# Stored partial sums loaded beside the gate tiles, and a regrouped staging of the output projection, in a hybrid retention and S5 layer

## The chip, the cores and the metric

The kernel runs on one core of a Trainium2 chip. The metric is the device time of one execution in microseconds (us): the median of three timed runs of the kernel before is 2620.29 us (2620.25 to 2623.68).

## The reference, cut to what matters

One layer serves 1024 prompt tokens and 8 sample tokens, 1032 columns in all. After an RMS norm one wide projection gives queries, keys, values, two S5 inputs and four gates. Two branches (retention and a diagonal state space) work on them, and the end of the layer, where the change lies, is

```python
yb = y * jax.nn.sigmoid(y @ w_glu + b_glu)            # inside the S5 branch
ya = (ya * silu(za)) @ w_pa                           # 1024 -> 2048
yb = (yb * silu(zb)) @ w_pb                           # 1024 -> 2048
merged = jax.nn.sigmoid(ga) * ya + jax.nn.sigmoid(gb) * yb
out = merged @ w_out                                  # 2048 -> 2048
return x + rmsnorm(out, g_post)
```

All of it is float32 (2048 wide model, 8 retention heads of 128, 64 S5 groups of 16).

## The kernel before, in words

**Products.** The big matrix products go over 2x2 blocks with seven products in place of eight: `product(g)` (L907) is one of them, `g // 7` is the step and `g % 7` the product in it. A step makes two row blocks of 128 outputs over a depth of 1024 (512 for each block of the 2x2 scheme). Each float32 operand is split into a high and a low float32r part (ACT copies the high part, DVE subtracts), and three matmuls stand for one. So a step before the output projection is 7 x 24 matmuls of 258 columns, and a step of the output projection is 7 x 12 of 324.

**Steps.** Steps 0 to 69 are the two depth halves of the wide projection, 70 to 73 `glu` (SG = 70), 74 to 81 `pa` (SA = 74), 82 to 89 `pb` (SB = 82), 90 to 97 and 98 to 105 the two depth halves `o0` and `o1` (SO = 90, SP = 98) of the output projection for the last 648 columns (TA = 384 to TOK = 1032). The first 384 columns follow in a last loop (from L1724) that uses the merged columns as the stationary operand and 512 wide pieces of `w_out`.

**Forms.** The right hand side of the seven products are seven forms of four tiles each (`FORMS`, L751). Three are parts of the source itself (`u1`, `v1`, `v2`), four are sums (`t1` to `t4`) that an earlier piece of work stores in device memory: `make_forms` (L1393) for `pb`, `forms_o` (L1480) for the output projection, which loads pairs of rows of `mg_d`, makes four DVE operations on each pair and stores two tiles to `fo_d`. `transition` (L1301) then loads ("stages") the 28 form tiles of a stage of work, one tile a DMA (`stage`, L840), and splits them (`unstage`, L859, through `split`, L258) during the last three steps before they are used: two loads in each of the first four products, as many as the pool `stg3` has buffers, then a load behind each split. The places `a0` to `a15` rotate (`qslot`, L828), and `forms_o` uses two places that are free meanwhile (`a6`, `a7` for `o0`; `a4`, `a5` for `o1`), two pairs of rows at a time, so the third and fourth pair overwrite the first and second.

**Gates.** In `pa` and `pb` an evacuated result tile `t` (128x516) is multiplied by its gate (`gated`, L1429), which `load_z` (L1423) has loaded on ACT's queue into `zz`. `pa` stores the product in `pap_d` (L1448). `pb` has DMA add `pap_d` into `t` (L1450, an accumulating DMA on POOL's queue) and four products later (LAG = 4) stores `t` to `mg_d` (L1451), also by POOL.

**Tiles in flight.** The evacuation tiles `p1`, `u2` and `u3` come from the pool `ev` with two buffers each, `st` from another with two; PSUM has three accumulators (`pst`). The weights `wr` come through SP's queue (`fetch`, L864) into seven buffers; `prep` (L880) forms the block sums and the splits two products ahead.

**What sets the order.** Each engine works through one list in order, and a wait at its head holds all behind it. The tile framework makes these lists from the program, and may bring an instruction forward past others of its engine; `issue_after` binds the background work (`slot`, `late_work`) only to instructions on PE, ACT, DVE and SP. POOL has no such anchor.

**The last loop.** `load_m` (L1528) loads 384 columns of a row of `mg_d`, `split_m` (L1531) splits them and loads the row four further; the first four loads are written at the start of the last step, the splits follow, one a product and then one a pass of the last loop. The norm weights `gb` and the residual rows `x_of(0)`, 1 MB each, are loaded by POOL ahead of that loop (L1702, L1703).

Of the kernel before, what the change touches and what calls it, by code (L numbers as in the profile page):

```python
# [10 lines left out]
F32 = mybir.dt.float32  # L11
# [7 lines left out]
D = 2048  # L19
SEQ = 1024  # L20
NB = 8
TOK = SEQ + NB
# [6 lines left out]
SW = TOK - TA  # L29
HO = SW // 2  # L30
THIRDS = [(0, 384), (384, 768), (768, TOK), (TA, TOK)]
HT = TOK // 2
# [47 lines left out]
def emit(ctx, tc, I, O):  # L80
    nc = tc.nc
    V, A, P, T = nc.vector, nc.scalar, nc.gpsimd, nc.tensor
# [7 lines left out]
    def add(out, a, b, eng=None):  # L90
        return tt(out, a, b, ALU.add, eng)
# [19 lines left out]
    act = ctx.enter_context(tc.tile_pool(name="act", bufs=1))  # L111
# [19 lines left out]
    pap_d = dram("pap_d", [16, 128, TOK])  # L131
# [16 lines left out]
    mg_d = dram("mg_d", [16, 128, TOK])  # L148
# [19 lines left out]
    bg = deque()  # L168
# [129 lines left out]
    def x_of(k):  # L298
        return xs[k][:, 0, :], xs[k][:, 1, :]
# [50 lines left out]
    with tc.tile_pool(name="start", bufs=3) as sp:  # L350
        ssq = sp.tile([128, TOK], F32, name="ssq", bufs=1)
        banks = [[mmbank() for _ in range(3)], [mmbank(), mmbank(), misc()]]
        w = None
# [449 lines left out]
    def popen(name, side, bufs):  # L803
        st = ExitStack()
        return st, st.enter_context(tc.tile_pool(name=name, bufs=bufs, side=side))
# [11 lines left out]
    lim = [7 * len(steps)]  # L817
# [117 lines left out]
    def at(g, f):  # L935
        due.setdefault(g, []).append(f)
# [359 lines left out]
        opened["fx"], opened["fxp"] = popen("fx", "left", 4)  # L1296

    def stg_open(bufs):
        opened["stg"], opened["stgp"] = popen("stg3", "left", bufs)

    def transition(g, base, kind, eng=P):  # L1301

        q = g - 7 * base
        n = moved.setdefault(kind, [0, 0])

        def load(eng=P):
            at(g, lambda o=order_q[n[0]]: stage(opened["stgp"], kind, *o, eng))
            n[0] += 1

        if 0 <= q < 4:  # L1310
            load(eng)
            load(eng)
        if 3 <= q < 20:
            for i in range(1 if q < 7 else 2):
                if n[1] < 28:
                    at(g, lambda o=order_q[n[1]]: unstage(kind, *o))
                    n[1] += 1
                    if n[0] < 28:
                        load()
# [73 lines left out]
    def make_forms(src, F):  # L1393

        t = {}

        def ld(i):
            t[i] = [opened["fxp"].tile([128, TOK], F32, name="fx") for _ in range(2)]
            for x, k in zip(t[i], (i, 4 + i)):
                P.dma_start(x, src[k])  # L1400

        ld(0)
        ld(1)
        for _ in range(3):
            yield
        for i in range(4):
            u, v = t.pop(i)
            mix_a(u, v)
            yield
            mix_b(u, v, F, i)  # L1410
            yield
            if i < 2:
                yield
                yield
                ld(i + 2)
                yield
        opened["fx"].close()


    zq = {}  # L1420
    AT = {"11": (0, 0), "22": (1, 1), "21": (1, 0), "12": (0, 1)}

    def load_z(s, name):  # L1423
        kind, p = steps[s]
        r, c = AT[name]
        zq[name] = zz_tile()
        A.dma_start(zq[name], {"glu": zy_d, "pa": sga_d, "pb": sgb_d}[kind][2 * p + r, :, HT * c:HT * c + HT])

    def gated(g, name, t, ps=None):  # L1429
        s = g // 7  # L1430
        kind, p = steps[s]
        r, c = AT[name]
        m, cols = 2 * p + r, slice(HT * c, HT * c + HT)
        z = zq.pop(name)
        if kind == "glu":
            def times():
                mul(t, t, z)
                P.dma_start(yb_d[m, :, cols], t)

            A.activation(t if ps is None else two(t), t if ps is None else ps, AF.Sigmoid, bias=bglu[:, m:m + 1])  # L1440
            at(g + 1, times)
            return
        if ps is None:
            mul(t, t, z)
        else:
            mul(two(t), ps, two(z))
        if kind == "pa":
            P.dma_start(pap_d[m, :, cols], t)  # L1448
        else:
            P.dma_start(t, pap_d[m, :, cols], accum_op=ALU.add)  # L1450
            at(g + LAG, lambda: P.dma_start(mg_d[m, :, cols], t))  # L1451
# [28 lines left out]
    def forms_o(kh, wait):  # L1480

        t, w = {}, {}

        def ld(i):
            if i < 2:
                w[i] = act.tile([128, 2, TOK], F32, name=f"a{(6, 4)[kh] + i}")
            t[i] = w[i % 2][:, 0, 0:SW], w[i % 2][:, 1, 0:SW]
            for x, k in zip(t[i], (8 * kh + i, 8 * kh + 4 + i)):
                P.dma_start(x, mg_d[k, :, TA:TOK])

        for i in range(4):
            if i % 2 == 0:
                if i:
                    yield
                ld(i)
                if i:
                    yield
                ld(i + 1)
                for _ in range(wait):
                    yield  # L1500
            u, v = t.pop(i)
            u1, u2, v1, v2 = u[:, 0:HO], u[:, HO:SW], v[:, 0:HO], v[:, HO:SW]
            sub(u1, u1, u2)
            sub(u2, u2, v2)
            yield
            add(v2, v2, u1)
            sub(v1, v1, v2)
            P.dma_start(fo_d[kh, 0, i], u)
            P.dma_start(fo_d[kh, 1, i], v)
            yield  # L1510

    flat_ = {}

# [14 lines left out]
    def load_m(m):  # L1528
        P.dma_start(spare(m), mg_d[m, :, 0:TA])

    def split_m(m):  # L1531
        split(merged(m), spare(m))
        if m + 4 < KD:
            load_m(m + 4)
# [121 lines left out]
    for s in range(SG, len(steps)):  # L1656
        kind, p = steps[s]
        if s in (SG + 1, SA + 1, SB + 1, SO + 1, SP + 1):
            opened["stg"].close()
        if s == SA + 1:  # L1660
            fx_open()
            bg.append(make_forms(yb_d, fb_d))
        if s == SB + 4:
            bg.append(forms_o(0, 2))
        if s in (SG + 2, SB - 2, SB + 6, SP - 2):
            drain()
            stg_open(8)
        if s == SO:
            zstack.close()
            bg.append(forms_o(1, 3))  # L1670
        if s == SO + 1:
            zrstack, zr0 = popen("zr", "left", 4)
            zrp = [zr0]
        if s == SP + 1:
            zr2stack, zr1 = popen("zr2", "left", 4)
            zrp.append(zr1)
            bg.append(rows_out())
        for n in range(7):
            g = now[0] = 7 * s + n
            if n == 1:  # L1680
                fetch(s + 1)
            prep(g + 2)
            (evac_p if s < SO else evac_o)(g, product(g))
            if n in (0, 2, 3, 4) and s < SO:
                at(g, lambda s=s, n=n: load_z(s, {0: "11", 2: "22", 3: "21", 4: "12"}[n]))
            transition(g, 2 * NP - 2, "glu")
            transition(g, SG + 2, "pa")
            transition(g, SB - 2, "pb")
            transition(g, SB + 6, "o0")
            transition(g, SP - 2, "o1")  # L1690
            if s == len(steps) - 1 and n > 4:
                raw_of["pool"] = wst
                next_w()
            if s == len(steps) - 1:
                for m in range(4) if not n else (n - 1,):
                    at(g, lambda m=m, n=n: split_m(m) if n else load_m(m))
            late_work(g)
            slot()
    small = const.tile([128, 24], F32, name="small")
    sm = [(small[:, o:o + 4], small[:, o + 4:o + 5], small[:, o + 5:o + 6], small[:, o + 6:o + 7]) for o in (0, 8, 16)]  # L1700
    gb = flat(1, "gb")[:, 0:D]
    P.dma_start(gb, bass.AP(tensor=I["g_post_row"].tensor, offset=I["g_post_row"].offset, ap=[[0, 128], [1, D]]))  # L1702
    P.dma_start(x_of(0), I["xB"][0])  # L1703

    def evac_c(g, c, ps):
        s4, r1, r2, r3 = sm[c]
# [17 lines left out]
    for g in range(4):  # L1724
        both_ = banks_of["pst"].tile([128, 2, 512], F32, name="acc")
        ps = [both_[:, 0, :], both_[:, 1, :], mmbank()]
        e = 11 if g == 3 else 13
        todo_ = [[(k, c) for c in range(3)] for k in range(e)] + [[(k, c) for k in range(e, KD)] for c in range(3)]
        for st in todo_:
            for k, c in st:  # L1730
                while order_w and order_w[0] <= (g, k + 1):
                    next_w()
                wh, wl = wb[g, k]
                xh, xl = (a[:, 128 * c:128 * c + 128] for a in merged(k))
                for a, b in ((xh, wh), (xh, wl), (xl, wh)):
                    anchor["p"] = T.matmul(ps[c], a, b, start=k == 0 and a is xh and b is wh, stop=k == KD - 1 and a is xl).ins  # L1736
                if k == KD - 1:
                    evac_c(g, c, ps[c])
            now[0] += 1
            if rest:  # L1740
                with ExitStack() as after:
                    for ins in anchor.values():
                        after.enter_context(tc.issue_after(ins))
                    split_m(rest.popleft())
            slot()
        if g == 2:
            drain()
# [81 lines left out]
```

## Time and profile before

| what | value |
|---|---|
| median of three runs | 2620.29 us |
| the profiled execution | 2619.01 us, span 2617.1 us |
| granted TensorE clock | 0.994 |
| PE busy, weight loads busy | 2565.9 us (98%), 2518.0 us (96%) |
| DVE, ACT, POOL busy | 1983.2 us (76%), 971.5 us (37%), 784.4 us (30%) |
| DMA moved | 519.09 MB, mean 198 GB/s |

The span runs from the first to the last instruction of the profiled execution; its own time is 1.9 us more. PE is busy in nearly all of the 40 slices of the profile but for two about 2200 us in (0.8 and 0.7) and the last (0.8). In the rows of the profile an engine's name with a q is its sequencer; the releaser of a wait is inferred from the semaphores.

### The profile page before, as it was taken

The page shows a single profiled execution, that of the slowest core. Times are in us where ns is not written, and L with a number is a line of the kernel's source. Part 1 is how long each engine was busy: PE and PEld are TensorE (multiplying, and loading weights), DVE is VectorE, ACT ScalarE, POOL GpSimd, SP SyncE. Part 2 cuts the span into 40 slices and gives each one's busy share as a digit, 9 for nine tenths or more (in the row PEclk, how much of TensorE's full clock was granted, in tenths as well). Part 3 has the DMA queues.
Part 4 walks back from the last instruction along what each step waited for, and adds up shares of the span by engine and source line. Part 5 has one row for each costly group of instructions (what it writes and reads, how often), then busy time and mean ns, then how long its engine had stood idle before and what let it go on. Part 6 is the DMA issues. An engine that isn't in the chain of part 4 may idle for free.

```text
span 2617.1 us, 52507 instructions
## 1 busy us (share of the span) xinstructions
PE 2565.9 (98%) x19948; PEld 2518.0 (96%) x19948; DVE 1983.2 (76%) x4159; ACT 971.5 (37%) x1747; POOL 784.4 (30%) x1300
## 2 busy tenths in 40 slices
PE   9999999999999999999999999999999998799998
PEld 8999999999999999999999999999999998799976
DVE  6655988889889877558877766668886866788875
ACT  6113233333323324343333444346532422345532
POOL 0103322222222222333244444335221323523320
PEclk9999999999999999999999999999999999999999
DMA  5886434434444447888879888889786879957784
GB/s 192 265 267 209 151 115 127 138 119 120 133 122 128 131 138 236 205 208 198 201 200 247 228 205 227 203 207 298 248 275 236 249 197 249 275 174 175 196 303 139
DMA packets 233500, 519.09 MB, mean 198 GB/s; under 512 B 33968, under 2 KB 61056, under 8 KB 232480
## 3 DMA queue, kind: packets, MB, share of 16 engines
q0 software_dynamic: 106464, 308.09, 42.9%
q1 hardware_dynamic: 91552, 159.30, 19.8%
q10 hardware_dynamic: 35232, 48.36, 5.9%
q8 instruction: 157, 2.57, 0.4%
q14 instruction: 95, 0.78, 0.1%
HBM read 342.36 MB, written 173.25 MB: 197 GB/s over the span
## 4 chain that ended last, share of the span: by engine, by line
PE 81%; issue 6%; DMA 6%; DVE 3%; POOL 3%; ACT 1%; POOLq 0%; DVEq 0%; ACTq 0%; SPq 0%
PE acc L919 63%; PE acc L1736 5%; PE mm L214 2%; PE mm L212 2%; PE mm L213 2%; DMA u<-pap_d 1%; DMA fo_d<-a 1%; DVE a L85 1%; DMA a<-mg_d 1%; DMA st<-pap_d 1%; PE misc L637 1%; PE misc L715 1%; PE misc L714 1%; DVE wlo L85 1%; PE misc L1133 1%
## 5 line engine op out<-in xcount | busy, mean ns | idle before, releaser
L919 PE MATMUL acc<-a,whi 128*128 128x258 f32 (+1 forms) x10976 | 1844.0, 287 | 30.9 <-DVE u L85 22.3
L919 PEld LDWEIGHTS acc<-a,whi 128*128 128x128 f32 x10976 | 1545.2, 190 | 39.3 <-ACT whi L900 12.2
L919 PE MATMUL acc<-a,wlo 128*128 128x258 f32 (+1 forms) x5488 | 1156.8, 285 | 0.5 <-DVE wlo L85 0.5
L919 PEld LDWEIGHTS acc<-a,wlo 128*128 128x128 f32 x5488 | 866.9, 190 | 1.0 <-DVE wlo L85 1.0
L900 ACT CAST whi<-wraw 128x512 fp32r<-128x512 f32 x424 | 263.2, 621 | 690.0 <-PE acc L919 512.4
L85 DVE TENSOR_TENSOR wlo<-wraw,whi 128x512 fp32r<-128x512 f32 x456 | 312.7, 686 | 173.3 <-ACT whi L900 114.2
L900 ACT CAST whi<-wr 128x512 fp32r<-128x512 f32 x318 | 197.3, 621 | 567.3 <-PE acc L919 511.1
L85 DVE TENSOR_TENSOR wlo<-wr,whi 128x512 fp32r<-128x512 f32 x380 | 260.7, 686 | 72.7 <-ACT whi L900 41.7
L212 PE MATMUL mm<-a,whi 128*128 128x384 f32 (+1 forms) x448 | 145.1, 326 | 5.6 <-ACT whi L205 5.6
L85 DVE TENSOR_TENSOR wraw<-wr 128x512 f32<-128x512 f32 x212 | 145.5, 686 | 2.7
L213 PE MATMUL mm<-a,whi 128*128 128x384 f32 (+1 forms) x448 | 145.2, 324 | 0.1
L214 PE MATMUL mm<-a,wlo 128*128 128x384 f32 (+1 forms) x448 | 144.8, 323 | 0.1
L85 DVE TENSOR_TENSOR a<-stg,a 128x516 fp32r<-128x516 f32 (+1 forms) x196 | 118.0, 632 | 32.2 <-ACT a L259 27.9
L259 ACT CAST a<-stg 128x516 fp32r<-128x516 f32 (+1 forms) x196 | 104.8, 574 | 48.5 <-DMA stg<-mg_d 17.8
L1736 PE MATMUL acc<-whi,a 128*128 128x512 f32 x372 | 117.8, 395 | 1.9 <-ACT whi L205 1.9
L85 DVE TENSOR_TENSOR u<-acc,p 128x516 f32<-128x516 f32 (+1 forms) x106 | 70.1, 661 | 57.3 <-PE acc L919 56.7
L85 DVE TENSOR_TENSOR u<-acc,u 128x516 f32<-128x516 f32 (+1 forms) x100 | 67.3, 673 | 58.7 <-PE acc L919 57.7
L85 DVE TENSOR_TENSOR p<-acc,p 128x516 f32<-128x516 f32 (+1 forms) x100 | 67.2, 672 | 53.3 <-PE acc L919 53.2
L973 POOL DMA_DIRECT2D u<-pt_d x70 | 61.6, 881 | 117.7 <-DVE u L85 79.5
L85 DVE TENSOR_TENSOR u<-p,acc 128x516 f32<-128x516 f32 (+1 forms) x106 | 69.7, 657 | 32.5 <-PE acc L919 12.9
L971 POOL DMA_DIRECT2D pt_d<-u x70 | 38.6, 552 | 179.7 <-DVE u L85 129.7
L212 PEld LDWEIGHTS mm<-a,whi 128*128 128x128 f32 x448 | 84.5, 189 | 5.8 <-ACT whi L205 5.6
(395 smaller groups left out, 3080.8 us busy)
## 6 DMA issues: line engine op xcount, KB each, us to landing
wr<-in_w_in SPq DMA_DIRECT2D x280, 256.0 KB
pt_d<-u POOLq DMA_DIRECT2D x70, 258.0 KB, 3.1
u<-pt_d POOLq DMA_DIRECT2D x70, 258.0 KB, 5.0
wr<-in_w_out SPq DMA_DIRECT2D x64, 256.0 KB
wr<-in_w_outB SPq DMA_DIRECT2D x64, 256.0 KB
stg<-fm_d POOLq DMA_DIRECT2D x44, 258.0 KB, 4.4
pt_d<-st POOLq DMA_DIRECT2D x35, 258.0 KB, 3.2
pt_d<-p POOLq DMA_DIRECT2D x35, 258.0 KB, 3.1
```

Of the source, the lines that this page charges most:

```text
L85: return (eng or V).tensor_tensor(out, a, b, op)
L212: T.matmul(ps, wh[:, i, :], xh[:, t0:t1], start=first, stop=False)
L213: T.matmul(ps, wh[:, i, :], xl[:, t0:t1], start=False, stop=False)
L214: anchor["p"] = T.matmul(ps, wl[:, i, :], xh[:, t0:t1], start=False, stop=last).ins
L259: A.copy(dst[0], src)
L637: T.matmul(ps[0:16, g * 128:(g + 1) * 128], B1[:, g, :], W3[:, g, 0:8, :], start=True, stop=True)
L714: T.matmul(o, Tm[:, g, :], U[:, g, 0:136], start=True, stop=False)
L900: anchor["a"] = A.copy(hi, f).ins
L919: anchor["p"] = T.matmul(o, a[:, i, :], x, start=first and i == 0 and a is wh and b is xh, stop=n in (2, 5, 6) and i == 3 and a is wl, ski ...
L971: P.dma_start(pt, t)
L973: P.dma_start(t, pt, accum_op=ALU.add)
L1736: anchor["p"] = T.matmul(ps[c], a, b, start=k == 0 and a is xh and b is wh, stop=k == KD - 1 and a is xl).ins
```

## The change

- `pb`, from its third step on: `load_z` also loads the partial sum from `pap_d` into a new pool `pp` (four buffers, ACT's queue). `gated` adds it on DVE and stores `t` to `mg_d` at once. The first two steps keep the accumulating DMA.
- `forms_o`: two places hold six tiles, so that three pairs of rows fit; the first two pairs are loaded together, the third two background turns later, the fourth after the second pair's store. The turns waited ahead of the first pair are 3 (was 2) for `o0` and 6 (was 3) for `o1`.
- `transition`: as many first loads as there are buffers, 6 for `o0` and 11 for `o1` (8 and 8 before), and these first loads go through SP's queue for both.
- The four first `load_m` are written one step earlier; `gb` and `x_of(0)` are loaded in the last loop, after its 10th and 21st pass.

```diff
-        n = moved.setdefault(kind, [0, 0])
+        n = moved.setdefault(kind, [0, 0, 0])
...
-        if 0 <= q < 4:
-            load(eng)
-            load(eng)
+        if q == 0:
+            n[2] = opened["n"]
+        for _ in range(2):
+            if 0 <= q and n[2]:
+                n[2] -= 1
+                load(eng)
...
         A.dma_start(zq[name], {"glu": zy_d, "pa": sga_d, "pb": sgb_d}[kind][2 * p + r, :, HT * c:HT * c + HT])
+        if kind == "pb" and p > 1:
+            zq[name, "p"] = ppp.tile([128, HT], F32, name="pp")
+            A.dma_start(zq[name, "p"], pap_d[2 * p + r, :, HT * c:HT * c + HT])
...
+        elif (name, "p") in zq:
+            add(t, t, zq.pop((name, "p")))
+            P.dma_start(mg_d[m, :, cols], t)
         else:
             P.dma_start(t, pap_d[m, :, cols], accum_op=ALU.add)
             at(g + LAG, lambda: P.dma_start(mg_d[m, :, cols], t))
...
         def ld(i):
-            if i < 2:
-                w[i] = act.tile([128, 2, TOK], F32, name=f"a{(6, 4)[kh] + i}")
-            t[i] = w[i % 2][:, 0, 0:SW], w[i % 2][:, 1, 0:SW]
+            a, b = w[0], w[1]
+            t[i] = {0: a[0:2], 1: b[0:2], 2: (a[2], b[2]), 3: a[0:2]}[i]
...
+        for j in range(2):
+            f = act.tile([128, 4 * HT], F32, name=f"a{(6, 4)[kh] + j}")
+            w[j] = [f[:, SW * i:SW * i + SW] for i in range(3)]
+        ld(0)
+        ld(1)
+        for n in range(wait):
+            yield
+            if n == 1:
+                ld(2)
...
+            if i == 1:
+                ld(3)
+                for _ in range(wait - 3):
+                    yield
...
+        if s == SB + 1:
+            ppstack, ppp = popen("pp", "left", 4)
+        if s == SO + 1:
+            ppstack.close()
         if s == SB + 4:
-            bg.append(forms_o(0, 2))
+            bg.append(forms_o(0, 3))
...
-            stg_open(8)
+            stg_open({SB + 6: 6, SP - 2: 11}.get(s, 8))
...
-            bg.append(forms_o(1, 3))
+            bg.append(forms_o(1, 6))
...
-            transition(g, SB + 6, "o0")
-            transition(g, SP - 2, "o1")
+            transition(g, SB + 6, "o0", nc.sync)
+            transition(g, SP - 2, "o1", nc.sync)
...
-                for m in range(4) if not n else (n - 1,):
-                    at(g, lambda m=m, n=n: split_m(m) if n else load_m(m))
+                if n:
+                    at(g, lambda m=n - 1: split_m(m))
+            if s == len(steps) - 2 and n > 2:
+                at(g, lambda m=n - 3: load_m(m))
...
+            if now[0] == lim[0] + 9:
+                P.dma_start(gb, bass.AP(tensor=I["g_post_row"].tensor, offset=I["g_post_row"].offset, ap=[[0, 128], [1, D]]))
+            if now[0] == lim[0] + 20:
+                P.dma_start(x_of(0), I["xB"][0])
```

More of the change, by code (lines that the diff above doesn't have):

```diff
@@ L1298, in stg_open @@
     def stg_open(bufs):
+        opened["n"] = bufs
         opened["stg"], opened["stgp"] = popen("stg3", "left", bufs)
@@ L1484, in ld @@
         def ld(i):
-            if i < 2:
-                w[i] = act.tile([128, 2, TOK], F32, name=f"a{(6, 4)[kh] + i}")
-            t[i] = w[i % 2][:, 0, 0:SW], w[i % 2][:, 1, 0:SW]
+            a, b = w[0], w[1]
+            t[i] = {0: a[0:2], 1: b[0:2], 2: (a[2], b[2]), 3: a[0:2]}[i]
             for x, k in zip(t[i], (8 * kh + i, 8 * kh + 4 + i)):
                 P.dma_start(x, mg_d[k, :, TA:TOK])
-        for i in range(4):
[L1492 to L1500, printed above, removed]
+        for j in range(2):
[7 more added lines that the diff above has]
+                ld(2)
+        for i in range(4):
             u, v = t.pop(i)
@@ L1701, in emit @@
     gb = flat(1, "gb")[:, 0:D]
-    P.dma_start(gb, bass.AP(tensor=I["g_post_row"].tensor, offset=I["g_post_row"].offset, ap=[[0, 128], [1, D]]))
-    P.dma_start(x_of(0), I["xB"][0])
     def evac_c(g, c, ps):
```

## The prediction, made before the changed kernel ran

> **What bounds the kernel now.** I read the page first: how busy PE is, and the chain of work that ended last.
>
> ```profile
> PE 2565.9 (98%) x19948; PEld 2518.0 (96%) x19948; DVE 1983.2 (76%) x4159; ACT 971.5 (37%) x1747; POOL 784.4 (30%) x1300
> ...
> PE 81%; issue 6%; DMA 6%; DVE 3%; POOL 3%; ACT 1%; POOLq 0%; DVEq 0%; ACTq 0%; SPq 0%
> ```
>
> PE is busy 98% of the span, so nothing that only unloads another engine pays, and nothing but the 51 us in which PE is idle (2617.1 less 2565.9), with the slow matmuls behind them, is to be had. The chain in order of time says where. Columns: start, length, what.
>
> ```profile
> 1778.42 250.85 PE acc L919 x2088
> ...
> 2291.22 59.17 PE acc L919 x395
> ```
>
> Up to 2029 and from 2291 the chain is matmul after matmul; between the two rows it has only one longer stretch of PE. Third, the busy times by stage. Columns: window, length, busy time and instructions of PE, PEld, DVE, ACT, POOL, granted clock, DMA share, GB/s. The first row is one undisturbed step of `pb` (84); then steps 86 and 87; 88 and 89; 90 to 92 of `o0`; one undisturbed step of `o0` (93); steps 97 and 98 to 99 (`o0` to `o1`).
>
> ```profile
> 2101.10:2121.30 20.20, 20.20 (x171) 20.20 (x170) 13.05 (x20) 4.88 (x9) 5.09 (x8) 1.00 0.85 215
> 2141.40:2195.10 53.70, 45.03 (x339) 44.65 (x338) 29.38 (x50) 9.83 (x17) 19.92 (x31) 0.90 0.87 228
> 2195.10:2249.70 54.60, 43.46 (x338) 42.33 (x337) 33.14 (x59) 15.68 (x32) 22.96 (x36) 0.94 0.89 241
> 2249.70:2298.60 48.90, 40.68 (x255) 39.05 (x254) 41.31 (x81) 19.42 (x40) 26.45 (x47) 0.97 0.91 295
> 2298.60:2311.10 12.50, 12.50 (x87) 12.50 (x86) 9.56 (x16) 5.00 (x9) 3.77 (x7) 1.00 0.58 185
> 2348.60:2361.10 12.50, 12.50 (x86) 12.50 (x86) 12.05 (x25) 8.90 (x20) 7.62 (x15) 1.00 0.82 250
> 2361.10:2391.20 30.10, 27.74 (x169) 26.41 (x168) 25.69 (x49) 16.08 (x35) 12.14 (x19) 0.94 0.73 195
> ```
>
> A step of `pb` takes 20.2 us and one of `o0` or `o1` 12.5 us when nothing holds PE. So steps 86 and 87 lose 53.7 - 40.4 = 13.3, 88 and 89 lose 54.6 - 40.4 = 14.2, 90 to 92 lose 48.9 - 37.5 = 11.4: 38.9 us. Steps 98 and 99 lose 30.1 - 25.0 = 5.1. The loss is more than PE's idle time (13.3 against 53.7 - 45.03 = 8.7 in the first): the clock column stands at 0.90 there, the matmuls behind a pause run slowly. A pause is paid for twice.
>
> Fourth, who waited for whom from 2060 to 2300. Columns: total us, times, longest.
>
> ```profile
> POOL mg_d L1451 <- DMA st<-pap_d: 35.1, 8, 5.8
> POOL mg_d L1451 <- DMA u<-pap_d: 34.0, 15, 5.8
> POOL mg_d L1451 <- DMA p<-pap_d: 24.1, 7, 5.4
> DVE a L85 <- ACT a L259: 23.3, 10, 5.6
> PE acc L919 <- DVE u L85: 22.0, 8, 7.5
> DVE a L85 <- DMA a<-mg_d: 18.4, 6, 5.2
> ...
> ACT a L259 <- DMA fo_d<-a: 13.0, 2, 7.9
> ```
>
> POOL stands 93.2 us (35.1 + 34.0 + 24.1) ahead of the stores to `mg_d`, until an accumulation from `pap_d` has landed. How that looks on POOL:
>
> ```profile
> 2132.86 0.56 POOL L1451 DMA_DIRECT2D mg_d<-st  x1 [5.82 <-DMA st<-pap_d]
> 2133.40 0.90 POOL L1450 DMA_DIRECT2D u<-pap_d  x1
> 2140.16 0.56 POOL L1451 DMA_DIRECT2D mg_d<-u  x1 [5.85 <-DMA u<-pap_d]
> ...
> 2157.72 0.56 POOL L1451 DMA_DIRECT2D mg_d<-st  x1 [4.87 <-DMA st<-pap_d]
> ```
>
> Issue, wait, store, issue: a round of four tiles, from one `st` store to the next, takes 2157.72 - 2132.86 = 24.9 us in a step of 20.2, so POOL falls 4.7 us further behind in every step. The tiles `p1`, `u2` and `u3` aren't stored when their buffers are wanted two steps later, the evacuation waits, and PE waits for it (22.0 us on DVE). The loads for the forms stand in the same queue and come late, so DVE waits for them (18.4 us); their stores come late too, and the first splits for `o0`, which overwrite `a6` and `a7`, wait for those (13.0 us).
>
> **The change part by part.** *Partial sums by a load and a DVE add, 24 of the 32 tiles.* POOL loses 24 accumulations and the waits behind them and keeps four stores of 0.56 us a step. The 8 accumulations of steps 82 and 83 stay; what they leave behind is worked off from step 84 on. Added are 24 loads on ACT's queue and 24 adds on DVE.
>
> ```profile
> L1427 ACTq DMA_DIRECT2D zz<-sgb_d x32: 326/326/327, 2060.7 to 2240.7; - x32
> ```
>
> ```profile
> L85 DVE TENSOR_TENSOR a<-stg,a 128x324 fp32r<-128x324 f32 x56 | 26.2, 491 | 25.1 <-ACT a L259 25.0
> ...
> L85 DVE TENSOR_TENSOR u<-u,zz 128x516 f32<-128x516 f32 x5 | 3.4, 688 | 0.0
> ```
>
> Four more issues of 0.33 us are 1.3 us a step on ACT, which is busy 4.88 of 20.2: hidden; without that cover they would cost 24 x 0.33 = 7.8 us. What is queued behind such a load, should it wait for a free `pp` buffer, is the next copy of weights, for which PE waits; four buffers for four tiles a step are as many as `zz` has, and no row of the waits shows DVE waiting for `zz`, so I take no wait. The adds are 4 x 0.69 = 2.75 us a step: 13.05 + 2.75 = 15.8 of 20.2, hidden in steps 84 to 87. In step 89 they are not, where the splits for `o0` run: two a product, 14 x 0.49 = 6.9, makes 22.7 of 20.2.
>
> *How much of 38.9 us comes back.* With POOL's waits gone, the tiles are stored in time, and the pair loads and their stores come before they are needed. What is late next? Two things bound it from above. First DMA:
>
> ```profile
> 2000.30:2020.40 20.10, 20.10 (x170) 20.10 (x169) 13.04 (x20) 4.78 (x8) 2.10 (x5) 1.00 0.50 159
> 2140.00:2300.00 160.00, 131.97 (x948) 128.83 (x947) 105.68 (x193) 45.55 (x88) 71.50 (x117) 0.94 0.88 251
> ```
>
> The stretch holds 0.88 x 160 = 141 us of DMA time. A step of `pa` (first row) has the traffic of a step of `pb` but for the accumulations: 0.85 - 0.50 over 20.2 us is 7.1, or 1.8 us for each of four, while a plain tile of 128x516 floats costs 0.26 MB / 159 GB/s x 0.50 = 0.8. The change saves some 0.95 us for each of 16 tiles here: 141 - 15 = 126 us. PE alone would need 160 - 38.9 = 121. So 5 us stay by DMA. Second DVE: the same crowd of splits runs in steps 97 to 99, without the adds, and loses 5.1 there, of which 3.5 is another wait (below). So 1.6 stays, and 2.75 for the adds of step 89. I add the two bounds up, 5 + 1.6 + 2.75 = 9.4, though they may overlap: 38.9 - 9.4 = 29.5 us come back. The ends for this term: 38.9 if DMA and DVE keep up, and 19 if DMA takes all its 141 us.
>
> *Six places, the waits of 3 and 6 turns.* The third pair no longer waits for the first pair's store; only the fourth does. Its price is in the term above: no more than the longest wait of DVE for `a<-mg_d`, 5.2 us, less the product (2.88 or 1.8 us) by which the accumulators run ahead. I take nothing more for it, since its load goes out a store earlier than now.
>
> *First loads by the weights' queue, 6 and 11 buffers.* For `o0` six buffers are three products of 2.88 us ahead, later three of 1.8; I take nothing, the DMA bound covers it. For `o1` eleven buffers bring the last loads three splits earlier, 1.5 products or 2.7 us. Here is what was late:
>
> ```profile
> ACT a L259 <- DMA stg<-mg_d: 2.7, 1, 2.7
> ```
>
> ```profile
> 2362.57 0.54 POOL L1529 DMA_DIRECT2D a<-mg_d  x1
> ```
>
> ACT stood 2.7 us for the last tiles of `o1`, and the copies of weights behind it. In the row of 98 and 99 above PE idles 30.1 - 27.74 = 2.4 and loses 0.06 x 30.1 = 1.8 by the clock; I take 3.5 of the 5.1, between 0 and 5.1. Moved past on SP's queue are the weights: if a first load has to wait at its head, the weights behind it wait too. What stands for it that they can:
>
> ```profile
> SPq L876 <- DVE wraw L85: 215.5, 38, 12.2
> ```
>
> SP waits 215.5 us in 345 (2055 to 2400) for weight buffers to come free, so it is ahead of the need, and ACT's copies wait for no weights in that stretch. Cost taken: nothing.
>
> *The loads around the last loop.* The row of 2362.57 is a `load_m` that the program has in step 105, and the trace has it in step 98: POOL's list is not in the order of the program. So it is open whether the late `gb` and `x_of(0)` stay late. What they do now:
>
> ```profile
> ACT a L259 <- DMA a<-mg_d: 7.9, 3, 5.0
> ```
>
> ```profile
> PE acc L1736 <- ACT whi L205: 1.9, 1, 1.9
> ```
>
> ```profile
> 2468.74 0.86 POOL L1702 DMA_DIRECT2D a<-in_g_post_row  x1
> ```
>
> ```profile
> a<-in_g_post_row POOLq DMA_DIRECT2D x1, 1024.0 KB, 11.8
> ```
>
> ```profile
> 2494.76 109.84 PE acc L1736 x471
> ```
>
> ACT waits 7.9 us for the rows of `mg_d` that land beside the two 1 MB loads, and PE 1.9 behind it. If they really go later, these come back. If `gb` goes as late as written, it leaves after the 10th pass and is wanted after the 14th: four passes of 9 matmuls at 109.84 / 471 = 0.233 us are 8.4 us, `gb` takes 11.8: a loss of 3.4. Between 1.9 gained and 3.4 lost I take 1.1 gained, because the row that is nearest, the 2362.57 one, has POOL issue early.
>
> *Sum.* 29.5 + 3.5 + 1.1 = 34.1 us. From the profiled execution's 2619.0 that is 2584.9; the median of the runs is 1.3 above it, 2620.3, so I say 2586.2, rounded to 2586.
>
> **A rule that speaks against it.** The trace has POOL standing 93.2 us for landings, not issuing. The Trainium skill, DMA: Bandwidth & Descriptors, section Issuing engines are not separate DMA queues, says that DMAs of all issuing engines share the same 16 DMA engines, and that spreading them only saves the time to issue. By that rule the 24 moved loads and the first loads save issue time alone, off the chain, and the time would follow DMA's own work, which the first rival works out. It says nothing of a queue whose head waits for a landing, which is what the rows show.
>
> **The rivals.** *DMA is the bound.* If the stretch from 2140 to 2300 keeps its 141 us of DMA work and the DMA engines are what is short, it can't fall below 141: at most 160 - 141 = 19 us come back, 2619.0 - 19 + 1.3 = 2601. For it: the shares of 0.87 to 0.91 above. Against it: POOL's waits are longer than they would be without a line, and the accumulations cost twice a plain load.
>
> *The weights' queue is held.* The first loads on SP wait for stores: those of rows 2 and 3 of `mg_d` (still accumulated in step 83), two tiles of `fo_d` for `o0`, four for `o1`. That is eight waits at the head of the queue that brings all weights. The longest wait for a store of `fo_d` was 7.9 us and half of the two 13.0 is 6.5; were each passed on to PE in full, 8 x 6.5 = 52 against 34 won gives 2620.3 + 18 = 2638. It decides from 34.1 / 8 = 4.3 us a wait. Against it: SP's 215.5 us in hand.
>
> *Nothing changes.* POOL's list may come out so that its head still waits (the loads of the fourth pair, the 8 accumulations): 2620.
>
> **How the numbers follow.** The forecast gets 0.63 (its own range 2574, all 38.9 + 5.1 + 1.9 = 45.9 back, to 2595), the DMA rival 0.22, no change 0.06, the held queue 0.09. The range reaches from 2574 over the DMA rival to 2604, with 3 us of the last loop's loss on it; some 0.2 stays outside. Faster by over 0.2% (5.2 us, about what a measurement of this kernel can tell from no change) is 0.63 + 0.22 = 0.85, within 0.06, slower 0.09.
>
> **What would show it.** Right: from the step that starts at 2101 on no POOL wait for `pap_d` ahead of a store to `mg_d`; steps 86 and 87 at 20.2 us; the chain PE through the stretch but for steps 89 to 92; DVE over 0.95 busy there; no wait of ACT for `stg<-mg_d` in `o1`. Wrong: steps 86 or 87 above 21 us, ACT or DVE waiting for weights or `pp`, SP waiting for `mg_d` or `fo_d`, or a DMA share at 1.0 through the whole stretch.

## The result, and the profile after

| | before | after |
|---|---|---|
| median, four runs each | 2620.27 us (2616.25 to 2623.68) | 2585.32 us (2584.75 to 2586.02) |
| profiled execution | 2619.01 us, span 2617.1 us | 2585.8 us, span 2584.0 us |
| granted clock | 0.994 | 0.997 |

The ratio is 0.9867, with a 95% interval from 0.985 to 0.9884: 35 us less, or 33.2 between the two profiled executions.

The page of after, busy times and shares of the chain:

```profile
PE 2557.5 (99%) x19948; PEld 2510.7 (97%) x19948; DVE 1996.9 (77%) x4183; ACT 970.7 (38%) x1747; POOL 752.8 (29%) x1259
...
PE 86%; issue 5%; DMA 3%; DVE 3%; POOL 2%; ACT 1%; ACTq 0%; POOLq 0%; DVEq 0%; SPq 0%
```

PE has 26.5 us of idle time left (2584.0 less 2557.5) where it had 51. DVE has the 24 adds (4183 instructions for 4159). The chain of after in order of time, in the stretch that was broken before (start, length, what):

```profile
2127.52 89.85 PE acc L919 x744
...
2226.69 4.97 DMA stg<-fo_d
...
2233.20 0.50 DVE u L85
2233.83 7.13 PE acc L919 x36
2241.46 58.58 PE acc L919 x392
```

From 2127 to 2217, from step 85 to late in step 89, the chain is now matmuls and nothing else. It leaves PE only after that: the pause of PE that ends at 2233.83, in step 90, is reached from the landing of a staged tile of `fo_d`. The busy times by stage, columns as in the prediction: steps 86 and 87; 88 and 89; 90 to 92; 98 and 99; the last loop with what follows it; and step 89 alone.

```profile
2142.00:2182.40 40.40, 40.40 (x339) 40.40 (x338) 33.58 (x59) 9.65 (x17) 9.71 (x18) 1.00 0.90 301
2182.40:2222.90 40.50, 40.50 (x338) 40.34 (x337) 39.82 (x70) 16.77 (x34) 14.13 (x27) 1.00 0.89 287
2222.90:2264.50 41.60, 39.58 (x255) 39.07 (x254) 38.82 (x78) 18.00 (x37) 18.63 (x35) 0.96 0.89 294
2326.90:2353.80 26.90, 26.07 (x171) 25.01 (x170) 25.55 (x49) 15.85 (x35) 9.75 (x15) 1.00 0.76 195
2428.90:2584.00 155.10, 139.69 (x600) 110.82 (x598) 97.59 (x187) 51.90 (x102) 27.26 (x48) 0.96 0.69 226
2202.80:2222.90 20.10, 20.10 (x170) 20.10 (x169) 19.91 (x37) 10.28 (x22) 9.71 (x19) 1.00 0.95 303
```

And the last loop of before:

```profile
2466.30:2617.10 150.80, 137.90 (x601) 109.87 (x599) 97.64 (x187) 51.97 (x103) 27.39 (x48) 0.98 0.70 232
```

Read against 40.4, 40.4, 37.5 and 25.0 us for steps that nothing holds, after loses 0.0, 0.1, 4.1 and 1.9 us where before lost 13.3, 14.2, 11.4 and 5.1. That is 34.7 us back in steps 86 to 92 and 3.2 in 98 and 99, less 4.3 in the last loop (155.10 - 150.80) and 0.4 in step 85 (below): 33.2, as measured between the two. The stages account for the whole difference of these two executions.

The waits of after from 2060 to 2300 (who waited, for whom: total, times, longest):

```profile
POOL mg_d L1461 <- DMA u<-pap_d: 10.0, 4, 4.5
POOL mg_d L1461 <- DMA st<-pap_d: 9.9, 2, 5.2
...
POOL mg_d L1461 <- DMA p<-pap_d: 8.4, 2, 5.3
```

28.3 us in 8 waits, for 93.2 us in 30 before, and the last of these eight stores is issued at 2118.9, in step 84. In steps 85 to 92 POOL waits for none. PE's only wait above 0.2 us between 2100 and 2270 is this one:

```profile
PE acc L919 <- DVE u L85: 1.8, 1, 1.8
```

### The profile page after: what moved, and what is told of

It reads as the page before. It is cut to its first block, busy times and chain, and to the rows that moved or that the text cites. A ratio compares the mean times of both kernels' runs of the same rounds, so it can differ in the third digit from the quotient of the medians.

```text
span 2584.0 us, 52569 instructions
## 1 busy us (share of the span) xinstructions
PE 2557.5 (99%) x19948; PEld 2510.7 (97%) x19948; DVE 1996.9 (77%) x4183; ACT 970.7 (38%) x1747; POOL 752.8 (29%) x1259
## 4 chain that ended last, share of the span: by engine, by line
PE 86%; issue 5%; DMA 3%; DVE 3%; POOL 2%; ACT 1%; ACTq 0%; POOLq 0%; DVEq 0%; SPq 0%
PE acc L919 68%; PE acc L1753 4%; PE mm L214 3%; PE mm L212 3%; PE mm L213 2%; DMA u<-pap_d 1%; DVE a L85 1%; DVE wlo L85 1%; PE misc L637 1%; PE misc L715 1%; PE misc L714 1%; PE misc L1123 1%; PE misc L1133 1%; PE misc L1102 1%; PE misc L665 1%
## 5 line engine op out<-in xcount | busy, mean ns | idle before, releaser
L1753 PEld LDWEIGHTS acc<-whi,a 128*128 128x128 f32 x372 | 70.6, 190 | 20.9 <-ACT whi L205 4.2
```

## The experiments

**The theories.** A: the loss of before is POOL's head, which stands waiting for an accumulation to land while stores and loads that other engines need are queued behind it. B (the prediction's first rival): the loss is DMA's own work, of which accumulations cost twice a plain load. C: something else in the change does it (places, buffers, queue, last loop). For what is left in after: D, DVE's crowd of adds and splits about step 89; E, staged tiles that come late; F, the waits at the head of SP's queue.

The columns of losses are read as above, in us, from one profiled execution of each kernel; they hold to about 0.1 (step 85 against 20.2). The medians are of 4 runs, of no_sums of 10; the ratio goes against before on the same chip, whose median was 2618.44 to 2620.27. The runs were spread over several chips, so small differences between kernels are better read from the ratios and the stages.

| kernel | median us | ratio, 95% | 85 | 86-87 | 88-89 | 90-92 | 98-99 | last loop us |
|---|---|---|---|---|---|---|---|---|
| before | 2620.27 | 1 | 0.0 | 13.3 | 14.2 | 11.4 | 5.1 | 150.8 |
| after | 2585.32 | 0.9867 [0.985, 0.9884] | 0.4 | 0.0 | 0.1 | 4.1 | 1.9 | 155.1 |
| after_again | 2585.27 | 0.987 [0.9856, 0.9885] | 2.5 | -0.1 | -0.1 | 3.3 | 1.8 | 153.1 |
| stores_by_act | 2590.97 | 0.9887 [0.9865, 0.9908] | 0.0 | 4.6 | -0.1 | 6.7 | 3.4 | 152.6 |
| sums_only | 2587.69 | 0.9874 [0.9857, 0.9891] | 0.0 | 0.0 | -0.1 | 6.9 | 3.7 | 154.9 |
| no_sums | 2621.48 | 1.0004 [0.9993, 1.0015] | 0.0 | 21.6 | 14.7 | 6.3 | 1.9 | 152.9 |
| last_as_before | 2584.62 | 0.9864 [0.9845, 0.9883] | 2.7 | -0.1 | -0.1 | 3.5 | 1.9 | 156.5 |
| late_by_weights | 2582.43 | 0.9853 [0.9836, 0.987] | 3.8 | -0.1 | -0.1 | 3.0 | 1.9 | 149.9 |
| first_by_pool | 2581.62 | 0.9858 [0.9843, 0.9873] | 0.0 | -0.1 | -0.1 | 2.9 | 1.8 | 151.2 |
| no_adds_p7 | 2583.19 | 0.9865 [0.9849, 0.9882] | 1.4 | -0.1 | -0.1 | 2.3 | 1.9 | 152.1 |
| o0_eight | 2584.23 | 0.9868 [0.9853, 0.9882] | 3.6 | -0.1 | 0.3 | 1.2 | 1.9 | 151.5 |
| sums_by_pool | 2586.75 | 0.9877 [0.9861, 0.9894] | 5.4 | -0.1 | -0.1 | 4.5 | 1.8 | 150.6 |
| three_mended | 2575.09 | 0.9832 [0.9817, 0.9846] | 0.0 | 0.0 | 0.0 | 1.2 | 1.8 | 148.1 |
| all_sums | 2576.48 | 0.9836 [0.9821, 0.985] | 0.0 | -0.1 | -0.1 | 1.4 | 1.8 | 148.1 |

### The head of the queue without less DMA work: stores_by_act

On before. All 32 accumulations stay, and nothing else of the change is in it; only the store of each sum to `mg_d` goes to ACT's queue.

```diff
-            at(g + LAG, lambda: P.dma_start(mg_d[m, :, cols], t))
+            at(g + LAG, lambda: A.dma_start(mg_d[m, :, cols], t))
```

> The kernel before, with one edit: in pb the stores to mg_d that follow an accumulation are issued by ACT in place of POOL, four products later as before. All 32 accumulations stay, so the DMA work is the same to the byte. If POOL's head waiting for landings is what costs (the theory of the forecast), POOL is free of 93 us of waits and steps 86 to 89 come back: 2590 to 2602. If the DMA work of the accumulations is what costs (the first rival), nothing comes back: 2615 to 2622. If it is half and half, about 2608.

Measured 2590.97 us (2588.75 to 2593.82), 29 of the 35 us. Its steps 86 and 87, 88 and 89, 90 to 92:

```profile
2141.20:2186.20 45.00, 42.10 (x339) 41.92 (x338) 32.56 (x56) 9.58 (x17) 13.22 (x20) 0.96 0.99 271
2186.20:2226.50 40.30, 40.30 (x338) 40.30 (x337) 33.24 (x59) 16.49 (x35) 18.58 (x29) 1.00 1.01 287
2226.50:2270.70 44.20, 40.28 (x255) 39.02 (x254) 38.26 (x76) 18.32 (x37) 20.63 (x37) 0.96 0.92 300
```

The second row decides between A and B. It has every accumulation of before and a DMA share of 1.01, and PE is busy in all of its 40.3 us. From 2060 to 2300 POOL's largest wait is now for DVE, and none is for `pap_d`:

```profile
POOL u L1450 <- DVE u L85: 28.0, 11, 6.3
```

So the DMA work that the change removes was not what held PE; what held it was the store that had to wait at POOL's head. By B this kernel would have stayed at 2620. Nor did the move make the stores themselves much cheaper for DMA: share times length over steps 82 to 92 is 0.94 x 210.2 = 198 us here and 0.85 x 237.8 = 202 in before.

### The partial sums alone, and all else alone: sums_only, no_sums

The first is before with the load into `pp`, the add and the store at once, and the six staging buffers for `o0` that the memory asks for. The second is after without them; the accumulation stays, and its store follows three products later (not four).

```diff
...
-            at(g + LAG, lambda: P.dma_start(mg_d[m, :, cols], t))
+            at(g + 3, lambda: P.dma_start(mg_d[m, :, cols], t))
```

> The kernel before with the partial sums alone: loads beside the gates and DVE adds for steps 84 to 89 (and, for the room, six staging buffers for o0); forms, first loads by POOL, waits and the loads around the last loop as before. Queue-head theory: most of the 34.7 us that steps 86 to 92 gave back comes from this alone, 2585 to 2595. If the three places and the loads by the weights' queue were needed for it, less than half comes back: 2603 or more.

> The changed kernel without the partial sums: all 32 accumulations by POOL as before, the stores to mg_d by POOL three products later in place of four; forms, first loads by SP and the last loop as changed. Queue-head theory: POOL falls behind as before, and SP is now held as well by stores that come late: 2608 to 2625. If the forms and the first loads by SP carried the gain: 2585 to 2600.

Measured 2587.69 us (2586.61 to 2589.04) and 2621.48 us (2615.02 to 2626.78). The partial sums alone bring 32.4 us (2620.09 - 2587.69); all the rest, with POOL's head as it was, brings nothing that can be measured in the whole. The waits of no_sums say why:

```profile
POOL mg_d L1455 <- DMA u<-pap_d: 45.9, 15, 5.8
POOL mg_d L1455 <- DMA st<-pap_d: 40.5, 8, 6.8
POOL mg_d L1455 <- DMA p<-pap_d: 22.6, 7, 5.4
```

POOL stands 109.0 us for the landings, more than the 93.2 of before. Its row of steps 86 and 87:

```profile
2141.90:2203.90 62.00, 49.08 (x339) 48.18 (x338) 32.45 (x56) 9.68 (x17) 19.69 (x31) 0.83 0.81 212
```

These steps lose 21.6 us with a DMA share of 0.81, where after has 0.90 and loses nothing: DMA was waiting too. The rest of the change does show in its own stages: `o1` loses 1.9 in place of 5.1, and 90 to 92 lose 6.3 in place of 11.4, 8.3 together. Steps 86 and 87 lose the 8.3 again (21.6 - 13.3); the store that comes a product earlier may have its part in that, which this kernel can't tell from the rest.

### The loads of the last loop: last_as_before, late_by_weights

The first is after with `load_m`, `gb` and `x_of(0)` written where before has them. The second has `gb` and `x_of(0)` after the same passes as after, but in SP's queue and bound there behind the weights.

```diff
-            if now[0] == lim[0] + 9:
-                P.dma_start(gb, bass.AP(tensor=I["g_post_row"].tensor, offset=I["g_post_row"].offset, ap=[[0, 128], [1, D]]))
-            if now[0] == lim[0] + 20:
-                P.dma_start(x_of(0), I["xB"][0])
+            if now[0] in (lim[0] + 9, lim[0] + 20):
+                with tc.issue_after(anchor["s"]):
+                    if now[0] == lim[0] + 9:
+                        nc.sync.dma_start(gb, bass.AP(tensor=I["g_post_row"].tensor, offset=I["g_post_row"].offset, ap=[[0, 128], [1, D]]))
+                    else:
+                        nc.sync.dma_start(x_of(0), I["xB"][0])
```

> The changed kernel with the edits around the last loop undone (first four row loads written in the last step, gb and the residual rows written ahead of the loop). In the trace the changed kernel still issues both 1 MB loads 1 to 5 us after the last product, so writing them late did little. If the 4.3 us that the last loop lost come from that edit (gb now issued a little later, beside the rows that the splits wait for), this gives 2580 to 2582; if they come from the loop's luck with the DMA order or from what runs ahead of it, 2584 to 2587.

> The changed kernel with gb and the residual rows really late: issued on SP's queue and bound there behind the weights fetched at the 10th and 21st pass. If the 2.84 us pause, its slow matmuls (1.7) and 0.8 more come from the two 1 MB loads that land beside the rows of mg_d, they go: 2579 to 2582. If the late gb is not there in time for the first evacuation, DVE waits for it and PE loses up to 3.4: 2583 to 2588.

Measured 2584.62 us (2582.67 to 2588.49) and 2582.43 us (2580.78 to 2583.11). The first is after again: writing the loads later did nothing. POOL in after, about 2428.9, where the last loop begins:

```profile
2427.88 0.54 POOL L1760 DMA_DIRECT2D a<-in_xB  x1
...
2434.07 0.54 POOL L1758 DMA_DIRECT2D a<-in_g_post_row  x1
```

The load that is written behind the 21st pass is issued a microsecond ahead of the loop, and the one behind the 10th pass 5 us into it. ACT then waits 7.01 us for a row of `mg_d` that was in flight beside these two:

```profile
2441.00 0.51 ACT L259 CAST a<-a 128x384 fp32r<-128x384 f32 x1 [7.01 <-DMA a<-mg_d]
```

Bound to SP's list the norm weights leave 4 us into the loop (2434.67), so hardly otherwise than in after, and the residual rows 30 (2460.91). In the loop PE no longer waits for ACT (3.4 us in after, 1.5 to 3.4 in every execution with the residual rows issued early), and it takes 149.9 us:

```profile
2430.60:2580.50 149.90, 137.91 (x600) 109.81 (x599) 97.61 (x187) 52.43 (x103) 26.53 (x47) 0.98 0.69 233
```

### The first loads by POOL again: first_by_pool

```diff
-            transition(g, SB + 6, "o0", nc.sync)
-            transition(g, SP - 2, "o1", nc.sync)
+            transition(g, SB + 6, "o0")
+            transition(g, SP - 2, "o1")
```

> The changed kernel with the first loads of o0 and o1 (6 and 11 as there) issued by POOL again. In the changed kernel SP stood 14.2 us at its head for a store to mg_d from step 83, and ACT's gate load of step 85 was released only by the landing of that first load; PE paused 0.2 to 2.4 us there, and 1.7 more by slow matmuls where it was the longer pause. If that is the price of the weights' queue, step 85 is undisturbed and SP waits for weight buffers alone: 2583 to 2585. If POOL needs the relief (its waits for fo_d and mg_d at its head come back), steps 86 to 92 lose 2 to 6 us: 2587 to 2591.

Measured 2581.62 us (2580.06 to 2583.97), 3.7 below after by the medians and 2.4 by the ratios; the intervals of the two ratios overlap, so the size is not settled by these runs alone. The queue's waits on SP from 2055 to 2400, first in after, then without that edit:

```profile
SPq L876 <- DVE wraw L85: 153.7, 37, 11.1
SPq L876 <- DVE wlo L85: 81.5, 35, 14.3
SPq L857 <- DMA fo_d<-a: 27.1, 6, 11.4
SPq L857 <- DMA mg_d<-u: 24.2, 2, 14.2
```

```profile
SPq L876 <- DVE wraw L85: 202.9, 45, 11.2
SPq L876 <- DVE wlo L85: 107.7, 38, 13.8
```

In after SP stands eight times, 51.3 us, with a first load at its head that waits for a store, and behind it the weights; the time comes out of its reserve (310.6 us of waiting for free buffers without, 235.2 with). PE's waits for weights are 0.5 us in after over that stretch, and 0.8 without the edit. What can be seen of a loss lies in steps 84 and 85, first in a second run of after (after_again, below), then in this kernel:

```profile
2102.00:2144.70 42.70, 40.45 (x337) 40.23 (x336) 30.70 (x47) 9.41 (x17) 9.77 (x16) 1.00 0.88 267
```

```profile
2101.90:2142.20 40.30, 40.30 (x338) 40.30 (x338) 30.78 (x47) 9.65 (x17) 9.24 (x16) 1.00 0.89 270
```

The 2.4 us are one pause of PE, for an evacuation by ACT. The table's column for step 85 shows a loss in all seven executions with first loads by SP and loaded sums, from 0.4 to 5.4 us, and in none of the others. How ACT comes to be late is to be seen in after itself, where the pause was only 0.2 us. SP and ACT in step 85:

```profile
2121.20 0.80 SPq L857 DMA_DIRECT2D stg<-mg_d  x2
```

```profile
2121.39 0.62 ACT L900 CAST whi<-wr 128x512 fp32r<-128x512 f32 x1 [2.26 <-DVE p L85]
2125.21 0.33 ACTq L1431 DMA_DIRECT2D zz<-sgb_d  x1
...
2126.36 0.62 ACT L900 CAST whi<-wraw 128x512 fp32r<-128x512 f32 x1 [4.35 <-issue]
```

SP's head comes free at 2121.2 and issues two staged tiles (two more had left before the wait); ACT, done with its copy at 2122.0, issues the next gate load 3.2 us later, and copies and evacuations are queued behind it. The chain of after runs this way into PE's long stretch from 2127.52:

```profile
2118.86 2.33 DMA mg_d<-u
2121.63 3.56 DMA stg<-mg_d
2125.63 0.63 ACTq L1434
2126.88 0.59 ACT p L1467
```

So the gate load was released by the landing of the second of SP's two tiles, issued at 2121.63 and landed 3.56 us later, at 2125.19. What ties them are semaphores, the counters by which a landing is told: in the trace's records the DMAs of SP and ACT share eight of them (100, 102, 104 to 109), and POOL's use eight others (111 to 118). The gate load of 2125.21 waits for number 109, on which that staged tile counts as well, and leaves 0.02 us after it has landed. In no_sums SP's head is held just as long (14.6 us), but ACT, with no sums to load, issues its gate load on time (2121.74); the one that is tied to a staged tile comes later (2128.06), and step 85 loses nothing. In first_by_pool the staged tiles count on POOL's semaphores.

### What is left in steps 90 to 92: no_adds_p7, o0_eight

The first leaves out the four adds of step 89, so that the first branch is missing from two blocks of 128 rows of the merged sum. The second has eight staging buffers for `o0`, and three `pp` buffers to make room.

```diff
-            add(t, t, zq.pop((name, "p")))
+            if p < 7:
+                add(t, t, zq[name, "p"])
+            zq.pop((name, "p"))
```

```diff
-            ppstack, ppp = popen("pp", "left", 4)
+            ppstack, ppp = popen("pp", "left", 3)
...
-            stg_open({SB + 6: 6, SP - 2: 11}.get(s, 8))
+            stg_open({SB + 6: 8, SP - 2: 11}.get(s, 8))
```

> The changed kernel with the four DVE adds of step 89 left out (the loads of the partial sums stay, so the last 256 rows of the merged result lack one branch). DVE was busy 19.91 of 20.10 us in step 89 and steps 90 to 92 lost 4.0. If DVE's crowd causes that, 2.75 us less work takes away the pause of 1.8 and its slow matmuls: steps 90 to 92 lose 1 or less, 2581 to 2583. If ACT's three waits for staged tiles (3.3 us) cause it, it stays: 2584 to 2586.

> The changed kernel with eight staging buffers for o0 in place of six, and three buffers for the partial sums in place of four to make the room. If late staged tiles cause the 4.0 us of steps 90 to 92, they go: 2581 to 2583. If DVE is what is short there, they stay: 2584 to 2586. If three buffers for the sums are too few, DVE waits for them from step 84 on: above 2590.

Measured 2583.19 us (2580.73 to 2585.34) and 2584.23 us (2582.66 to 2585.98): neither differs from after by more than the runs scatter. Their rows of steps 90 to 92:

```profile
2223.30:2263.10 39.80, 38.02 (x254) 37.46 (x253) 37.30 (x75) 18.10 (x37) 18.31 (x35) 1.00 0.92 303
```

```profile
2226.20:2264.90 38.70, 38.17 (x254) 37.44 (x253) 38.37 (x78) 17.95 (x37) 17.51 (x33) 1.00 0.92 304
```

The loss falls from 4.1 (after) and 3.3 (after_again) to 2.3 without the adds and to 1.2 with the two more buffers and all the adds in place. In all three kernels with eight buffers it is 1.2 to 1.4, in all with six and every add 2.9 or more. The larger part is thus E, tiles that come late, as in the chain of after above, which reaches the pause from a staged tile of `fo_d`; but the two overlap, and how the 4 us divide stays open. Step 85 of o0_eight had a pause of its own (3.6 us lost), which is why its median shows so little.

### After again, and the sums by POOL's queue: after_again, sums_by_pool

after_again is the changed kernel with no edit, beside the next three on one chip. sums_by_pool issues the 24 plain loads by POOL, the engine that issued the accumulations.

```diff
-            A.dma_start(zq[name, "p"], pap_d[2 * p + r, :, HT * c:HT * c + HT])
+            P.dma_start(zq[name, "p"], pap_d[2 * p + r, :, HT * c:HT * c + HT])
```

> The changed kernel once more, unchanged, beside the next three: 2584 to 2587, with the pause of step 85 longer in some runs than in others.

> The changed kernel with the loads of the partial sums issued by POOL in place of ACT; they stay plain loads ahead of their use, and POOL has 24 more issues of 0.55 us. If what the sums won is the wait at POOL's head, the queue that loads them hardly matters: 2584 to 2590. If it is that POOL has less to issue, most of the gain goes: 2600 or more.

Measured 2585.27 us (2582.37 to 2589.32) and 2586.75 us (2586.45 to 2589.0). Which queue brings the partial sum makes no difference that can be told. What counts is that nothing waits for its landing at the head of a queue. In step 85 of sums_by_pool, which loses 5.4 us, the weights themselves come late: they are issued behind SP's held tiles at 2126.5, and DVE waits 6.2 us for them.

### The three edits that lost, undone: three_mended, all_sums

three_mended is first_by_pool, late_by_weights and o0_eight in one. all_sums (the diff is against three_mended) is that with the partial sums from the first step of `pb`, so that no accumulation is left (five staging buffers for `pb` make room, and the pool `pp` is opened earlier, which isn't shown).

```diff
-        if kind == "pb" and p > 1:
+        if kind == "pb":
...
-            stg_open({SB + 6: 8, SP - 2: 11}.get(s, 8))
+            stg_open({SB - 2: 5, SB + 6: 8, SP - 2: 11}.get(s, 8))
```

> The changed kernel with the three edits that won alone: first loads by POOL, gb and the residual rows really late behind the weights, eight staging buffers for o0 with three for the sums. They mend different places (step 85; the last loop; steps 90 to 92), so if the prices add up, 3.7 + 2.9 + 1 to 3 come off: 2576 to 2579. If the eight buffers only moved the loss, or the 1 MB loads on SP's queue hold weights: 2580 to 2583.

> As the kernel with the three mended places, and the partial sums loaded from the first step of pb on, so that no accumulation is left (five staging buffers for pb make the room). Steps 82 to 85 lose nothing in the kernel with first loads by POOL, so the 8 accumulations cost nothing on the path: as that kernel, within 1.5. If five buffers are too few for the change from pa to pb: 2 to 8 more.

Measured 2575.09 us (2574.88 to 2576.47) and 2576.48 us (2576.01 to 2577.09). Steps 90 to 92 of three_mended, and its last loop:

```profile
2221.90:2260.60 38.70, 38.17 (x255) 37.46 (x254) 38.39 (x78) 17.87 (x37) 20.16 (x38) 1.00 0.91 308
2424.90:2573.00 148.10, 137.49 (x601) 110.03 (x599) 97.89 (x187) 52.54 (x103) 26.68 (x47) 0.98 0.70 237
```

It is 10.2 us faster than after on the same chip, with intervals apart (0.9832 [0.9817, 0.9846] against 0.987 [0.9856, 0.9885]), and the fastest kernel here. The three edits alone had brought 3.7, 2.9 and 1.1, 7.7 together, but late_by_weights and o0_eight still had the pause of step 85 (3.8 and 3.6 us). By stages the two spans, 2583.7 us of after_again and 2573.0, differ by 5.0 us in the last loop, 2.5 in step 85, 2.1 in steps 90 to 92 and 1.0 ahead of step 82. In three_mended the eight accumulations that the change leaves in place cost nothing: steps 84 and 85 lose nothing with them, and all_sums gains nothing without (it loses 0.8 in steps 82 and 83, where it has five staging buffers). In after they do have a part, since the late store on which SP's head waited was itself held for one of their landings.

## Why the prediction was right, and where it was not

**The number.** 2586 was forecast and 2585.32 measured, but two terms were wrong, and they cancel: 5.2 us more came back in the stretch than forecast, and 5.4 less about the last loop. That the median lies within 1 us of the forecast is luck; that most of the loss comes back is not.

**POOL's head (the mechanism).** Right, and shown: stores_by_act takes only that away and gains 29 us with the same DMA work, and no_sums, all the rest of the change with POOL's head as it was, gains nothing. One sign was set too strictly: four of POOL's waits for `pap_d` still end after 2101, in step 84. The Trainium skill, DMA: Bandwidth & Descriptors, section Issuing engines are not separate DMA queues, by which only issue time is saved when DMAs are spread over engines, does not hold in stores_by_act, where the head of a queue had stood for a landing and the same DMAs, spread, gain 29 us; it does agree with sums_by_pool, where plain loads change engines for 1.5 us between medians.

**The DMA term, 5 us that were to stay.** This is the step that failed. It read the DMA share as work that must fit: 141 us less 15 against 121 for PE. But a share near 1 did not hold PE: 1.01 over 40.3 us in stores_by_act at full matmul speed, and 0.90 and 0.89 over steps 86 to 89 of after, for a loss of 0.1 us. Measured for that term: nothing in steps 86 to 89, and what stays in 90 to 92 falls from 4.1 to 1.2 with two more buffers, while the share there goes from 0.89 to 0.92. The saving of DMA work was sized rightly: share times length over steps 82 to 92 falls from 202 us to 0.88 x 203.5 = 179, some 0.96 us for each of 24 tiles, as forecast. It was not what bounded the time. The rival built on it, 2601, falls with it.

**The DVE term, 1.6 + 2.75.** Its size came out (4.35 forecast, 4.1 measured), but by chance: its place and its cause are right only in part. Step 89, which it costed at 22.7 of 20.2 us, has DVE busy 19.91 of 20.10 us and loses nothing; the loss lies behind it, in step 90, and eight staging buffers take most of it away with all the adds there. Without the adds of step 89 2.3 us stay.

**`o1`, 3.5 of 5.1.** Right: 3.2. It shows in no_sums too, alone, and as much with the first loads by POOL (first_by_pool), so SP's queue is not needed for it. Without those edits stores_by_act and sums_only lose 3.4 and 3.7.

**The last loop, 1.1 gained.** Wrong in sign: 4.3 lost (2.3 in after_again). The prediction had said that POOL's list is not in the order of the program and so weighted an early issue; the trace has the late loads early, and last_as_before shows that the edit did nothing. The error was to price that case at a gain. The loss is not the edit's either: sums_only and stores_by_act, which have the last loop of before, take 154.9 and 152.6 us for it. In late_by_weights, three_mended and all_sums, with the residual rows really late, the loop takes 149.9, 148.1 and 148.1, and PE waits for ACT in none of them. In the eleven other executions it takes 150.6 to 156.5, before's 150.8 among them, so part of the 4.3 is scatter from one execution to the next; what sets it within that range is not settled.

**The held queue.** Its mechanism happened just as the rival had it: eight waits, 51.3 us, 6.4 each where 6.5 was costed. What did not follow was its price. SP had its reserve, and PE paid 0.4 to 5.4 us in step 85 and not 52. In after it paid through ACT, by the semaphores that SP's and ACT's DMAs share, a path that the prediction had not looked for; in sums_by_pool it paid through late weights, as the rival had it.

## What to carry to other kernels

When an engine that only issues DMAs seems busy, look at what stands at the head of its queue: a store that waits there for a landing holds everything behind it, and moving that one wait elsewhere (a prefetch and an add on an engine with time to spare, or the store alone on a queue that comes by later) was worth more than the bytes. Don't put loads that wait for late stores into the queue that feeds the engine that bounds the kernel, even where it has time in hand, and look at which other queues' DMAs count on the same semaphores: a load that is held on one can hold the issue of another. A DMA that is written later in the program is only later on the chip if something binds it there.

## What the hardware showed beside that

Short pauses of PE can be paid for twice, or not. Behind the pause of 1.8 us in step 90 of after the granted clock stood at half for 3.47 us (the third number from the end of the row: 0.53), and behind one of 2.4 us in the last loop of first_by_pool it did not fall at all (1.00 over the 6 us that hold it):

```profile
2233.83:2237.30 3.47, 3.47 (x13) 3.47 (x14) 3.47 (x8) 1.87 (x4) 0.55 (x1) 0.53 0.86 287
```

```profile
2438.00:2444.00 6.00, 3.40 (x15) 2.56 (x15) 4.15 (x9) 4.70 (x11) 1.61 (x3) 1.00 0.97 354
```

The Trainium skill, TensorE: Matmul & The Clock Gate, section HAM oscillation — how this bites in real kernels, sets the limit for an idle gap at about 3.4 us; here a gap half as long was followed by the slow clock. Its section What's actually happening says that the window in which activity is watched runs free, which may let one short pause count and another not; no run here shows where the window stood.
